# Gate and up on the second half of the tokens: block 1 computed ahead of block 0

## The chip, the cores and the metric

The kernel runs on one core of a Trainium2 chip. The metric is the device time of one launch in microseconds (us), the median of several runs. One further launch was profiled; its page and its trace are read below.

## The reference, cut to what matters

One decoder layer on x of 1024 tokens by 1024 channels, all in float32: two token mixers (differential attention and a convolution module) with a gated merge, then a SwiGLU channel mixer. The change lies in the channel mixer:

```python
    h = rms_norm(x, ffn_norm_w[l])
    gt, up = jnp.split(h @ w_gate_up[l], 2, axis=-1)
    x = x + (jax.nn.silu(gt) * up) @ w_down[l]
```

The hidden width FF is 2816, so gate and up are 22 blocks of 128 columns each; h is 1024 by 1024.

## The kernel before, in words

**Precision.** Every matrix operand is held as two fp32r tiles, a rounded high part (a ScalarE cast, `split_hi`, line 120) and the rest (a VectorE subtraction, `split_lo`, line 125). A product takes three TensorE matmuls: high times high, high times low, low times high (`mm3`, lines 152 to 155; `product`, line 1611).

**Stages.** Input projections, convolution and attention, the two output projections, the merge and `w_out` come first. The last matmuls of `w_out` (tile `wo`) run at about 1095 to 1121 us of the span. Then the channel mixer starts: `rest_of_rows` normalizes and transposes token tiles 4 to 7 into `h2_hi` and `h2_lo` (`h_hi`, `h_lo` in the profile) while the first blocks run.

**Two plain blocks.** Blocks f = 0 and f = 1 of gate and up (`NSTD = 2`) are computed plainly, on tokens 0 to 511 (sb = 0) and on tokens 512 to 1023 (sb = 1). `gate(f, sb, w)` runs 24 matmuls into a `pg` bank and a Silu on ScalarE (line 1477, tile `fsg`); `up(f, sb, w, sg)` runs 24 more, multiplies on VectorE (line 1482) and stores the result (line 1484). The weights are W[0], W[1] (gate and up of block 0) and W[2], W[3] (gate and up of block 1). They are loaded once and used for both halves. W[0], W[1] and W[2] fill the three buffers of the `whi`/`wlo` pairs in the pool `wp`. W[3] has no place there: `fourth` (line 539) puts it into the memory of the later tile `T4h`.

**The other 20 blocks** use a scheme of seven half-size products in place of eight. It needs differences of the four quarters of h: `differences()` (line 1501) takes 16 VectorE subtractions (lines 1508 to 1511) and splits T1, T2, T3 and T4 into high and low parts, four casts and four subtractions each. T4 is written where W[3] lay, so it can be written only after the last matmul that reads `fourth`. For each block f, `prepare(f)` (line 1572) loads two raw weight tiles (`wraw`, two buffers, line 1578) and makes, on VectorE and ScalarE, the pairs A11/A12, S1/S2 and S3/S4 (each one `whi`/`wlo` buffer, so three for a block) and A22 (`sh`, `sl`). The sums behind S1 to S4 are lines 1593 to 1596 (tile `s`); A22 is split by lines 120 and 125. `pair(f, ...)` (line 1616) runs the seven products of 12 matmuls each: A11 and A12 with h, S2 with T2, S1 with T1, S3 with T3, S4 with h, A22 with T4. Between the products come short steps on ScalarE and VectorE: the copy of the first product (line 1623, tile `p`), which must be done before S2 times T2 adds into the same bank, then lines 1625, 1626, 1630 and so on. `weight_sums` (lines 514 to 523, tile `wd`) prepares the down projection at the same time, one piece a block.

**What sets the order.** A scheduler places the instructions of each engine; each engine then works through its own list in order, and so does the DMA queue of SyncE (SP). An instruction that waits holds up all that stand behind it on its engine. A `whi`/`wlo` or `wraw` buffer goes to the next user when its last reader is done. After the 20 blocks comes the down projection (line 497).

Of the kernel before, what the change touches and what calls it, by code (L numbers as in the profile page):

```python
# [57 lines left out]
def kernel(  # L58
# [53 lines left out]
    def nm(s):  # L112
        uid[0] += 1
        return f"{s}_{uid[0]}"
# [4 lines left out]
    def split_hi(dst, src):  # L119
        act.copy(dst, src)  # L120
# [3 lines left out]
    def split_lo(dst, src, hi):  # L124
        last_lo[0] = dve.tensor_tensor(dst, src, f32(hi), op=ALU.subtract).ins  # L125
# [243 lines left out]
    def gemm_T(w, mhi, mlo, sb, amid=None):  # L369

        o = pg()
        cs = slice(sb * 512, (sb + 1) * 512)
        for k in range(NKT):
            mm3(o[:], w[0][:, k, :], w[1][:, k, :], kt(mhi, k)[:, cs], kt(mlo, k)[:, cs], k == 0, k == NKT - 1)
            if amid is not None and k == NKT // 2 - 1:
                amid()
        return o
# [1090 lines left out]
    def rest_of_rows(t_):  # L1468
        with after(last_mm[0]):
            norm2(t_, r2[1], tr_second)  # L1470
# [3 lines left out]
    def gate(f, sb, w, amid=None):  # L1474
        og = gemm_T(w, h2_hi, h2_lo, sb, amid)
        sg = wp.tile([P, 512], F32, tag="sg", name=nm("fsg"), bufs=2)
        act.activation(sg[:], og[:], AF.Silu)
        return sg

    def up(f, sb, w, sg, amid=None):  # L1480
        ou = gemm_T(w, h2_hi, h2_lo, sb, amid)
        dve.tensor_tensor(sg[:], ou[:], sg[:], op=ALU.mult)
        z = f"{sb + 1}{f % 2 + 1}"
        nc.sync.dma_start(sd[z][0][:] if z in sd else g21_d[:], sg[:])

    W = [ws.next()]
    sg = gate(0, 0, W[0])
# [4 lines left out]
    sg = gate(1, 0, W[2], lambda: rest_of_rows(5))  # L1492
# [8 lines left out]
    def differences():  # L1501


        q = []
        for i in range(4):
            b11, b21 = xa[i][:, 0:512], xa[i][:, 512:1024]
            b12, b22 = xa[4 + i][:, 0:512], xa[4 + i][:, 512:1024]
            dve.tensor_tensor(b11, b12, b11, op=ALU.subtract)
            dve.tensor_tensor(b12, b22, b12, op=ALU.subtract)
            dve.tensor_tensor(b22, b22, b11, op=ALU.subtract)  # L1510
            dve.tensor_tensor(b21, b21, b22, op=ALU.subtract)
            q.append({2: b22, 1: b11, 3: b12, 4: b21})
        for z in (2, 1, 3, 4):
            for i in range(4):
                ts = slice(i * P, (i + 1) * P)
                src = q[i][z].rearrange("p (k s) -> p k s", s=P)
                split_hi(T[z][0][:, :, ts], src)
                split_lo(T[z][1][:, :, ts], src, T[z][0][:, :, ts])

    sg = gate(0, 1, W[0])  # L1520
    up(0, 1, W[1], sg)
    differences()
    sg = gate(1, 1, W[2])
    up(1, 1, W[3], sg)
    n2_ctx.close()
    xp_ctx.close()

# [229 lines left out]
```

## Time and profile before

| | us |
|---|---|
| median of 3 runs (lowest to highest) | 1768.91 (1768.19 to 1770.76) |
| the profiled execution | 1769.82 |
| its span | 1768.0 |
| TensorE (PE) busy | 1740.1 |
| VectorE (DVE) busy | 1273.1 |
| ScalarE (ACT) busy | 800.8 |

The profiled execution's time is 1.82 us longer than its span. TensorE is the engine that is nearly always busy, so its idle stretches are what to look for. In a timeline row stand the start, the duration, the engine, the line, the operation, output and inputs, a count, and in brackets the idle time of that engine just before, with what ended it. The start-to-start distance of two 512-column matmuls that run without a wait is 0.227 us, although each shows 0.39 us: they overlap. PEclk is the granted TensorE clock, 1.00 being full speed.

### The profile page before, as it was taken

What the parts mean: (1) busy time and instruction counts of PE and PEld (TensorE: products, weight loads), DVE (VectorE), ACT (ScalarE), POOL (GpSimd) and SP (SyncE); (2) the same over time, 40 slices, a digit from 0 to 9 for tenths busy, and PEclk for the clock granted to TensorE, in tenths of its full rate; (3) what the DMA queues carried; (4) which work ended last, traced back from release to release, by engine and by line L of the source; (5) the groups of instructions that cost most, each with busy time, mean ns of one, the idle gap of its engine ahead of it and who ended that gap; (6) DMA issues with size and microseconds to landing.
All of it is one profiled execution on the core that took longest, in us unless ns stands there. A gap on an engine that the chain in (4) does not pass through costs nothing.

```text
span 1768.0 us, 25005 instructions
## 1 busy us (share of the span) xinstructions
PE 1740.1 (98%) x8983; PEld 1484.6 (84%) x8983; DVE 1273.1 (72%) x2171; ACT 800.8 (45%) x1883; POOL 19.6 (1%) x92
## 2 busy tenths in 40 slices
PE   6999999999999999999999999999999999999999
PEld 5778898998999998987788888878888888888887
DVE  6598888998898888885677534867667666665544
ACT  5221141557767776754457313633333333333332
POOL 0000000000000000000000000000000000000000
PEclk9999999999999999999999999999999999999999
DMA  6337334235443244341973544224544544697663
GB/s 231 107 125 232 131 111 115 70 104 138 120 141 105 82 125 145 97 147 60 339 261 108 167 166 143 90 90 152 171 159 148 177 153 148 202 357 250 214 214 131
DMA packets 251110, 275.29 MB, mean 156 GB/s; under 512 B 16505, under 2 KB 166050, under 8 KB 250986
## 3 DMA queue, kind: packets, MB, share of 16 engines
q1 hardware_dynamic: 249130, 267.47, 47.0%
q0 software_dynamic: 1280, 4.91, 0.9%
q10 hardware_dynamic: 576, 1.31, 0.3%
q8 instruction: 71, 1.16, 0.3%
q14 instruction: 53, 0.43, 0.1%
HBM read 176.59 MB, written 78.68 MB: 144 GB/s over the span
## 4 chain that ended last, share of the span: by engine, by line
PE 91%; DMA 3%; DVE 2%; ACT 2%; issue 1%; SPq 0%; DVEq 0%; ACTq 0%
PE acc L1611 19%; PE pg L153 14%; PE pg L154 14%; PE pg L155 14%; PE acc L497 12%; PE pg L688 4%; PE sc L1053 2%; PE sc L1052 2%; PE pT L1088 2%; PE wo L154 2%; PE wo L153 2%; PE wo L155 2%; PE pW L155 1%; PE pW L153 1%; PE pW L154 1%
## 5 line engine op out<-in xcount | busy, mean ns | idle before, releaser
L569 DVE SCALAR_TENSOR_TENSOR acc<-u,cw,acc 128x1024 f32<-128x1024 f32 x240 | 306.9, 1279 | 2.9
L153 PE MATMUL pg<-hT_hi,whi 128*128 128x512 f32 x512 | 201.7, 394 | 0.5 <-ACT hT_hi L120 0.2
L154 PE MATMUL pg<-hT_lo,whi 128*128 128x512 f32 x512 | 200.9, 392 | 0.0
L155 PE MATMUL pg<-hT_hi,wlo 128*128 128x512 f32 x512 | 200.7, 392 | 0.0
L120 ACT CAST whi<-wraw 128x1024 fp32r<-128x1024 f32 x101 | 106.1, 1051 | 182.9 <-PE pg L154 99.5
L125 DVE TENSOR_TENSOR wlo<-wraw,whi 128x1024 fp32r<-128x1024 f32 x101 | 123.0, 1219 | 63.3 <-ACT whi L120 59.4
L125 DVE TENSOR_TENSOR wlo<-draw,whi 128x1024 fp32r<-128x1024 f32 x75 | 91.8, 1224 | 89.1 <-ACT whi L120 86.1
L153 PE MATMUL pg<-whi,hT_hi 128*128 128x256 f32 x512 | 146.0, 285 | 0.3 <-ACT jk L756 0.3
L155 PE MATMUL pg<-whi,hT_lo 128*128 128x256 f32 x512 | 145.8, 285 | 0.0
L154 PE MATMUL pg<-wlo,hT_hi 128*128 128x256 f32 x512 | 145.5, 284 | 0.0
L120 ACT CAST whi<-draw 128x1024 fp32r<-128x1024 f32 x75 | 79.1, 1055 | 129.5 <-PE acc L497 122.6
L1059 ACT ACTIVATE E<-E,mn 128x256 f32<-128x256 f32 (+7 forms) x128 | 99.6, 780 | 45.9 <-DVE mn L1054 44.7
L497 PE MATMUL acc<-wlo,whi 128*128 128x512 f32 x308 | 119.8, 389 | 0.0
L497 PE MATMUL acc<-whi,wlo 128*128 128x512 f32 x308 | 119.8, 389 | 0.0
L153 PEld LDWEIGHTS pg<-hT_hi,whi 128*128 128x128 f32 x512 | 96.2, 188 | 20.5 <-ACT sgg L603 0.7
L155 PEld LDWEIGHTS pg<-hT_hi,wlo 128*128 128x128 f32 x512 | 96.2, 188 | 19.1
L154 PEld LDWEIGHTS pg<-hT_lo,whi 128*128 128x128 f32 x512 | 96.2, 188 | 19.0 <-issue 0.6
L153 PEld LDWEIGHTS pg<-whi,hT_hi 128*128 128x128 f32 x512 | 97.7, 191 | 2.2 <-ACT jk L756 1.0
L154 PEld LDWEIGHTS pg<-wlo,hT_hi 128*128 128x128 f32 x512 | 97.7, 191 | 1.3
L155 PEld LDWEIGHTS pg<-whi,hT_lo 128*128 128x128 f32 x512 | 97.7, 191 | 0.4
L1611 PE MATMUL acc<-h_hi,whi 128*128 128x512 f32 x240 | 93.4, 389 | 0.0
L1611 PE MATMUL acc<-h_lo,whi 128*128 128x512 f32 x240 | 93.4, 389 | 0.0
(280 smaller groups left out, 4191.1 us busy)
## 6 DMA issues: line engine op xcount, KB each, us to landing
wraw<-in_w_gate_up_dram SPq DMA_DIRECT2D x44, 512.0 KB, 4.8
wraw<-in_w_in_dram SPq DMA_DIRECT2D x38, 512.0 KB, 4.2
qs<-qs SPq DMA_DIRECT2D x96, 128.0 KB, 2.3
wd<-in_w_down_dram SPq DMA_DIRECT2D x44, 256.0 KB, 3.2
tdT<-wd SPq DMA_DIRECT2D x88, 128.0 KB, 4.5
draw<-sdS SPq DMA_DIRECT2D x44, 256.0 KB, 2.6
draw<-tdT SPq DMA_DIRECT2D x44, 256.0 KB, 4.3
wraw<-in_w_in_dram SPq DMA_DIRECT2D x32, 256.0 KB, 3.4
```

What stands on the lines that cost most here:

```text
L120: act.copy(dst, src)
L125: last_lo[0] = dve.tensor_tensor(dst, src, f32(hi), op=ALU.subtract).ins
L153: pe.matmul(o, lh, rh, start=start, stop=False)
L154: pe.matmul(o, lh, rl, start=False, stop=False)
L155: last_mm[0] = pe.matmul(o, ll, rh, start=False, stop=stop).ins
L497: m = pe.matmul(o[s_][i][:], l_[:, ts], r_[:, 512:], start=start and j + y_ == 0, stop=j == n - 1 and y_ == 2, skip_group_check=not start,)
L569: dve.scalar_tensor_tensor(acc[0][:], us[c][:, t : t + S], cw[:, c, t : t + 1], acc[0][:], op0=ALU.mult, op1=ALU.add)
L688: last_mm[0] = pe.matmul(o[:], l_, r_, start=first and n_ == 0, stop=last and n_ == len(terms) - 1).ins
L1052: pe.matmul(o[:, :w], qh[:, qs], k, start=True, stop=False)
L1053: last_mm[0] = pe.matmul(o[:, :w], ql[:, qs], k, start=False, stop=True).ins
L1059: act.activation(e[:, :nk], e[:, :nk], AF.Exp, bias=mn[:, j : j + 1], scale=-1.0, accum_out=l[:, j : j + 1])
L1611: pe.matmul(o[:], a_[x_][:, k, :], b_[y_][:, k, :], start=start and k + x_ + y_ == 0, stop=k == 3 and x_ == 1, skip_group_check=not start,)
```

## The change

On the second half of the tokens, gate and up of block 1 are computed first, then `differences()` is written, then gate and up of block 0. No computation is added or left out.

```diff
+    sg = gate(1, 1, W[2])
+    up(1, 1, W[3], sg)
+    differences()
     sg = gate(0, 1, W[0])
     up(0, 1, W[1], sg)
-    differences()
-    sg = gate(1, 1, W[2])
-    up(1, 1, W[3], sg)
     n2_ctx.close()
```

On TensorE the second half now runs through W[2], W[3] (`fourth`), W[0], W[1], where it was W[0], W[1], W[2], W[3]. As before, two matmuls of block 2's first product stand after the second of these four groups and three after the third.

The first place is on VectorE, where the plain blocks end. `fsg_11837` is the multiplication of the third plain group pair (up of the block that comes first on the second half), `fsg_11939` that of the last; T4l are the low parts of T4.

```order
 L125 TENSOR_TENSOR T2l<-xa_10937,T2h 128x4x128
 L1482 TENSOR_TENSOR fsg_11837<-pg_11839,fsg_11837 128x512
-L1482 TENSOR_TENSOR fsg_11939<-pg_11941,fsg_11939 128x512
 L125 TENSOR_TENSOR T4l<-xa_10938,T4h 128x4x128
 L125 TENSOR_TENSOR T4l<-xa_10939,T4h 128x4x128
```

The last multiplication no longer stands ahead of T4 and of all that follows T4.

The second place is on VectorE some ten instructions later. `wlo_11988` is the low part of block 2's S1/S2, `wlo_11992` of its S3/S4, `wlo_12037` of block 3's A11/A12; `s_1749`, `s_1750` and `sl_12124` belong to block 3.

```order
 L125 TENSOR_TENSOR wlo_11988<-s_1733_11977,whi_11987 128x1024
-L125 TENSOR_TENSOR wlo_11992<-s_1734_11978,whi_11991 128x1024
-L125 TENSOR_TENSOR wlo_12037<-wraw_11999,whi_12036 128x1024
 L1593 TENSOR_TENSOR s_1749_12034<-wraw_12001 128x512
-L1595 TENSOR_TENSOR s_1750_12035<-wraw_11999,wraw_12001 128x512
 L125 TENSOR_TENSOR sl_12124<-wraw_12001,sh_12123 128x512
 L518 TENSOR_TENSOR wd_12127<-wd_12127 128x256
 L1594 TENSOR_TENSOR s_1749_12034<-s_1749_12034,wraw_11999 128x512
+L1482 TENSOR_TENSOR fsg_11939<-pg_11941,fsg_11939 128x512
+L125 TENSOR_TENSOR wlo_11992<-s_1734_11978,whi_11991 128x1024
```

The last multiplication and block 2's S3/S4 now stand behind four steps of the next blocks, of which the first needs the raw tile `wraw_12001`.

The third place is on ScalarE at the same time. `whi_11987` is the high part of block 2's S1/S2, `whi_11991` of S3/S4, `sh_12123` the high part of block 3's A22, made from `wraw_12001`; `p_1748_12018` is the copy of block 2's first product.

```order
 L120 CAST sh_11995<-wraw_11975 128x512
+L1477 ACTIVATE fsg_11939<-pg_11914 128x512
+L120 CAST whi_11987<-s_1733_11977 128x1024
+L120 CAST sh_12123<-wraw_12001 128x512
+L120 CAST whi_11991<-s_1734_11978 128x1024
 L1623 COPY p_1748_12018<-acc_12004 128x512
-L120 CAST whi_11987<-s_1733_11977 128x1024
+L120 CAST whi_12036<-wraw_11999 128x1024
 L1626 ACTIVATE p_1748_12018<-p_1748_12018 128x512
```

S1/S2 moved ahead of the copy of the first product, and so did a cast that waits for a load.

## Prediction

> **What bounds the kernel now.** I read the page first: which engine is busy, and which ends the run.
>
> ```profile
> PE 1740.1 (98%) x8983; PEld 1484.6 (84%) x8983; DVE 1273.1 (72%) x2171; ACT 800.8 (45%) x1883; POOL 19.6 (1%) x92
> PE 91%; DMA 3%; DVE 2%; ACT 2%; issue 1%; SPq 0%; DVEq 0%; ACTq 0%
> ```
>
> TensorE is the bound. A change of order can only gain where TensorE stands still or runs slowly, so next the busy time by stage around the change and behind it (columns: stretch, its length, PE, PEld, DVE, ACT, POOL busy, PEclk, DMA share, GB/s).
>
> ```profile
> 1121.00:1200.00 79.00, 76.37 (x344) 62.47 (x343) 60.11 (x104) 37.79 (x63) 0.00 (x0) 0.98 0.28 90
> 1200.00:1560.00 360.00, 359.92 (x1588) 297.79 (x1587) 237.18 (x358) 122.25 (x167) 0.00 (x0) 1.00 0.53 171
> ```
>
> In the stage of the change TensorE is idle for 2.6 us and its mean clock is below 1; behind it TensorE is busy for 359.92 of 360 us. So whatever TensorE gets back here is not waited away later: the end moves with it. The waits of TensorE name the one place, and the timeline shows it.
>
> ```profile
> PE acc L1611 <- ACT whi L120: 2.4, 1, 2.4
> ```
>
> ```profile
> 1169.69 0.39 PE L1611 MATMUL acc<-h_hi,wlo 128*128 128x512 f32 x1
> ...
> 1173.77 0.39 PE L1611 MATMUL acc<-h_hi,wlo 128*128 128x512 f32 x1
> 1176.58 0.50 PE L1611 MATMUL acc<-T2h,whi 128*128 128x512 f32 x1 [2.42 <-ACT whi L120]
> ...
> 1177.84 0.80 PE L1611 MATMUL acc<-T2h,wlo 128*128 128x512 f32 x1
> 1178.43 0.63 PE L1611 MATMUL acc<-T2h,whi 128*128 128x512 f32 x1
> ...
> 1180.99 0.46 PE L1611 MATMUL acc<-T2h,whi 128*128 128x512 f32 x1
> 1181.29 0.39 PE L1611 MATMUL acc<-T2l,whi 128*128 128x512 f32 x1
> ...
> 1184.04 0.39 PE L1611 MATMUL acc<-h_hi,whi 128*128 128x512 f32 x1
> ```
>
> Block 2's first two products end at 1174.0 (1173.77 + 0.227), and the next product cannot start until 1176.58, since the high part of S1/S2 is late. Then a second loss: from 1177.84 to 1181.29 eight matmuls take 3.45 us where 1.81 us is usual (8 x 0.227). The stage table, cut finer, says why.
>
> ```profile
> 1163.00:1169.00 6.00, 6.00 (x28) 4.96 (x27) 0.00 (x0) 0.60 (x1) 0.00 (x0) 1.00 0.00 0
> 1169.00:1172.00 3.00, 3.00 (x15) 2.48 (x14) 2.06 (x4) 2.11 (x5) 0.00 (x0) 1.00 0.18 69
> ...
> 1174.00:1176.50 2.50, 0.16 (x1) 0.00 (x0) 2.50 (x5) 1.02 (x2) 0.00 (x0) 1.00 0.22 70
> 1177.80:1179.50 1.70, 1.66 (x4) 1.38 (x5) 1.22 (x1) 0.65 (x2) 0.00 (x0) 0.50 0.75 204
> 1179.50:1181.00 1.50, 1.50 (x5) 1.13 (x5) 0.88 (x1) 0.59 (x1) 0.00 (x0) 0.50 0.60 174
> ```
>
> After the idle stretch the granted clock is halved for about 3.3 us. The whole loss: from 1169.69 to 1184.04 stand 43 matmuls (19 of the first two products, 24 of S1 and S2), 43 x 0.227 = 9.75 us, but 14.35 us pass. **Loss 4.6 us**: 2.6 of idle, 1.65 of half clock, 0.35 of a refill and a short wait for `wlo` at 1177.84.
>
> Who made S1/S2 late? ScalarE and VectorE in the same microseconds:
>
> ```profile
> 1169.89 2.19 ACT L120 CAST T4h<-xa 128x512 fp32r<-128x512 f32 x4 [5.52 <-PE pg L155]
> 1171.98 0.62 ACT L120 CAST sh<-wraw 128x512 fp32r<-128x512 f32 x1
> 1175.48 1.05 ACT L120 CAST whi<-s 128x1024 fp32r<-128x1024 f32 x1 [2.41 <-DVE s L1594]
> ```
>
> ```profile
> 1158.70 0.68 DVE L1482 TENSOR_TENSOR fsg<-pg,fsg 128x512 f32<-128x512 f32 x1
> 1169.94 0.69 DVE L1482 TENSOR_TENSOR fsg<-pg,fsg 128x512 f32<-128x512 f32 x1 [10.57 <-issue]
> 1170.55 2.49 DVE L125 TENSOR_TENSOR T4l<-xa,T4h 128x512 fp32r<-128x512 f32 x4
> 1172.96 0.68 DVE L1593 TENSOR_TENSOR s<-wraw 128x512 f32<-128x512 f32 x1
> 1173.56 0.68 DVE L1595 TENSOR_TENSOR s<-wraw,wraw 128x512 f32<-128x512 f32 x1
> 1174.16 0.68 DVE L125 TENSOR_TENSOR sl<-wraw,sh 128x512 fp32r<-128x512 f32 x1
> 1174.77 0.68 DVE L1594 TENSOR_TENSOR s<-s,wraw 128x512 f32<-128x512 f32 x1
> 1175.97 0.68 DVE L1596 TENSOR_TENSOR s<-wraw,s 128x512 f32<-128x512 f32 x1
> 1176.57 1.22 DVE L125 TENSOR_TENSOR wlo<-s,whi 128x1024 fp32r<-128x1024 f32 x1
> ```
>
> VectorE idles 10.57 us, then works without a gap from 1169.94: the last multiplication, four T4 parts, then the sums, in steps of 0.6 us. All of it starts when the last plain group has been multiplied, because that group reads `fourth`, which lies where T4 goes, and its `fsg` stands at the head of the queue. The sums need nothing of it; they stand behind it.
>
> **The change, part by part.** Where TensorE stands between the four plain groups:
>
> ```profile
> 1157.67 0.39 PE L1611 MATMUL acc<-h_hi,whi 128*128 128x512 f32 x1
> 1163.57 0.39 PE L1611 MATMUL acc<-h_hi,wlo 128*128 128x512 f32 x1
> ```
>
> The groups end at 1157.67 (second), 1163.57 (third) and 1169.69 (fourth). All have 24 matmuls, so these times stay; no matmul is added or removed, and the swap itself costs nothing: the four weight tiles were all made for the first half.
>
> *T4 and the sums move forward.* `fourth` is now read last at 1157.45, one step before 1157.67. Before, T4h began 0.43 us after that matmul (its last was at 1169.46, one step before 1169.69; T4h at 1169.89). So T4h runs from 1157.9 to 1160.1 on a ScalarE that was waiting. VectorE is free at 1159.3, 0.6 after the 1158.70 row; four T4 parts end at 1161.7, and L1593, L1595, `sl`, L1594, L1596 follow to 1164.7. That is 11.25 us earlier for the first of them (1172.96 to 1161.7), in the idle 10.57 us.
>
> *S1/S2.* Its buffer is now the one of W[0], read until 1163.57, and its cast stands behind the Silu of that group: 1163.8 + 0.6 = 1164.4, cast until 1165.4, low part until 1166.7. TensorE asks for the high part at 1169.69 + 19 x 0.227 = 1174.0 and for the low part two matmuls on. Margins of 8.6 and 7.8 us: the 2.6 us wait goes, and with it what followed from it. **Minus 4.6 us** by this execution.
>
> *Multiplication, store and S3/S4 move back.* S3/S4 takes W[1]'s buffer, free only at 1169.9, and stands on ScalarE behind `sh_12123` and on VectorE behind `s_1749`; both wait for block 3's second raw tile. So does the last `fsg`, which nobody needs soon (its bank and its store have no reader in the next blocks). What stands behind that load on ScalarE is the copy of block 2's first product, on VectorE `wlo` of block 3's A11/A12. The load is priced by its rows of now:
>
> ```profile
> 1174.87 9.32 SPq L1578 DMA_DIRECT2D wraw<-in_w_gate_up_dram  x3
> ```
>
> ```profile
> 1181.84 0.62 ACT L120 CAST sh<-wraw 128x512 fp32r<-128x512 f32 x1 [1.75 <-DMA wraw<-in_w_gate_up_dram]
> ```
>
> ```profile
> DMA to landing us min/median/max: 2.9/4.2/8.4
> ```
>
> The first of three issues comes as `sl` ends (1174.84). I put the second at the end of L1596 (1176.65), which frees its buffer; used at 1181.84, that is 5.2 us. After the change L1596 ends at 1164.8, so the tile is there at 1170.0. ScalarE: `sh` 0.5, S3/S4 1.0, copy 0.6, done at 1172.1; T2's first matmul needs it at 1174.0 + 10 x 0.227 = 1176.3 (T1's first ten now go first). Margin 4.2 us. VectorE from 1170.0 to the end of `wlo_12037`: seven half-width steps of 0.6, two wide ones of 1.2, and three `wd` steps,
>
> ```profile
> 1183.72 0.42 DVE L518 TENSOR_TENSOR wd<-wd 128x256 f32<-128x256 f32 x1
> ```
>
> at about 0.35, in all 7.6: 1177.6. TensorE asks for it after the 24 matmuls of S1/S2 and four more, 1174.0 + 28 x 0.227 = 1180.35. Margin 2.7 us. It would be gone with a landing of 7.9 us, and the longest in the trace, 8.4, would cost 0.5 us. S3/S4 itself is ready at 1174, needed after 1183. Cost taken: 0; bounds 0 to 0.5 us. A gain beyond 4.6 is excluded: of the stage's 79.00 - 76.37 = 2.63 us of idle TensorE, 2.42 are this stretch.
>
> **Sum.** 1769.82 - 4.6 = 1765.2 for the profiled execution; its time lies 0.9 above the median of the runs, and from the median it is 1764.3. How far the half clock is in the median run is not known (below); I take **1764.9**, 4.0 us or 0.23% below 1768.91.
>
> [...] Three idle stretches of similar length:
>
> ```profile
> 28.49 1.29 PE L673 MATMUL px<-ident,xt 128*128 128x128 f32 x8 [2.17 <-DVE xt L667]
> 819.74 1.94 PE L1088 MATMUL pT<-ident,E 128*128 128x128 f32 x8 [3.15 <-DVE E L1068]
> ...
> 28.00:30.00 2.00, 1.47 (x10) 1.25 (x11) 1.83 (x4) 0.77 (x2) 0.00 (x0) 1.00 0.24 76
> 820.00:825.00 5.00, 4.88 (x23) 4.48 (x22) 2.04 (x4) 2.40 (x8) 0.20 (x1) 0.50 0.34 114
> ```
>
> After 2.17 us the clock stayed at 1.00, after 2.42 and 3.15 it was 0.50. So 2.42 us is near the point where it turns, and another execution may go the other way. [...]
>
> **Rivals.**
> 1. *The 2.42 us of idle do not halve the clock in the median run of before:* the gain is 4.6 - 1.65 = 2.95 us, 1766.0, within 0.2%. For it: the 2.17 row, and runs that spread over 2.6 us, more than 1.65. Against it: the profiled execution has it, and the idle is longer than 2.17. [...]
> 2. *The change gives back what it gains.* The buffer or the queue makes S1/S2 or block 3's A11/A12 late, TensorE waits 1 to 4 us in 1170 to 1185: 1767 to 1769. Against it: margins of 7.8 and 2.7 us. A version of it is that S1/S2 was late for another reason; but ScalarE's wait names L1594, and that step stood in an unbroken queue.
> 3. *Slower.* The load of `wraw_12001` now holds both queues. If it lands more than 7.9 us after its buffer is free, block 3's A11/A12 is late by the excess; to pass the old loss of 4.6 by 3.6 us, with 1.65 of half clock, the excess must be 6.5 us: a landing of 14.4 us, 1772.5. Against it: 8.4 is the longest of all landings, and the DMA engines have little else to do there (a share of 0.00 from 1163 to 1169, 0.18 to 1172).
>
> **How the numbers follow.** About 0.2% (3.5 us) is what a measurement of this kernel can tell from no change. Forecast (4.6 us or most of it, 1763.6 to 1765.4): 0.57. Rival 1: 0.31, rival 2: 0.08, both within 0.2%: 0.39. Rival 3: 0.04. The range: at the low end 4.6 off the lowest run and 0.3 for scatter, 1763.3; at the high end rival 1 from a run 1.2 above it, 1767.2; left out are rivals 2 and 3 and the tails, near 0.2.
>
> **What would show it.** Right: no TensorE wait at `acc` L1611 near 1174, clock 1.00 throughout 1170 to 1185, T4h at about 1158, the S1/S2 cast at about 1164.4, the 1184.04 matmul at about 1179.4. Wrong: a new wait at block 3's first product (1179 to 1181) or at T2's first matmul, `sh_12123` later than 1172, or a time of 1768 or more although the wait is gone, which would mean that the 4.6 us is lost again behind it.

## The result and the profile after

| | before | after |
|---|---|---|
| median of 7 runs on the same chip (lowest to highest) | 1770.76 us (1768.19 to 1772.96) | 1765.62 us (1763.01 to 1767.34) |
| profiled execution: time, span | 1769.82, 1768.0 us | 1765.62, 1763.6 us |
| the 43 matmuls of block 2's first products and S1/S2, in the profiled execution | 14.35 us | 9.75 us |

The measured ratio of after to before is 0.9974, 95% interval 0.9963 to 0.9985: 4.6 us faster, with 2.7 to 6.5 us as the interval (the shares times 1770.76; the two medians in the table are 5.1 us apart). A second measurement of the same kernel gave 0.9970, interval 0.9961 to 0.9979 (medians 1765.28 us against 1769.91). All gains below are worked out from such a ratio and the median of the kernel before that was measured beside it.

The page after: TensorE is still the bound, busy for 99% of the span, and the VectorE share of the chain that ended last fell from 2% to 1%.

```profile
PE 1737.5 (99%) x8983; PEld 1483.2 (84%) x8983; DVE 1273.4 (72%) x2171; ACT 802.9 (46%) x1883; POOL 19.6 (1%) x92
PE 93%; DMA 3%; ACT 2%; DVE 1%; issue 0%; SPq 0%; ACTq 0%
```

The stages around and behind the change, after (columns as before: stretch, length, PE, PEld, DVE, ACT, POOL busy, PEclk, DMA share, GB/s):

```profile
1121.00:1200.00 79.00, 78.86 (x364) 65.29 (x363) 63.36 (x110) 39.76 (x68) 0.00 (x0) 1.00 0.31 97
1200.00:1560.00 360.00, 359.94 (x1588) 297.74 (x1587) 238.16 (x357) 122.50 (x167) 0.00 (x0) 1.00 0.53 174
1160.00:1190.00 30.00, 30.00 (x134) 24.86 (x133) 17.71 (x28) 9.16 (x14) 0.00 (x0) 1.00 0.46 141
```

In the stage of the change the idle of TensorE went from 2.63 to 0.14 us and its mean clock from 0.98 to 1.00; behind it TensorE is as full as before (359.94 of 360). TensorE's timeline after, at the place where it stood still:

```profile
1169.87 0.39 PE L1611 MATMUL acc<-h_hi,wlo 128*128 128x512 f32 x1
...
1173.95 0.39 PE L1611 MATMUL acc<-h_hi,wlo 128*128 128x512 f32 x1
1174.18 0.39 PE L1611 MATMUL acc<-T1h,whi 128*128 128x512 f32 x1
...
1179.62 0.39 PE L1611 MATMUL acc<-h_hi,whi 128*128 128x512 f32 x1
```

The first S1/S2 matmul follows the last of the products at the usual 0.23 us. From 1169.87 to 1179.62 are 9.75 us for 43 matmuls, the bare work. ScalarE and VectorE after, as far as they lead there:

```profile
1158.06 2.19 ACT L120 CAST T4h<-xa 128x512 fp32r<-128x512 f32 x4 [2.56 <-PE pg L155]
...
1164.44 1.04 ACT L120 CAST whi<-s 128x1024 fp32r<-128x1024 f32 x1
1169.84 0.62 ACT L120 CAST sh<-wraw 128x512 fp32r<-128x512 f32 x1 [4.36 <-DMA wraw<-in_w_gate_up_dram]
...
1171.71 0.59 ACT L1623 COPY p<-acc 128x512 f32<-128x512 f32 x1 [0.29 <-PE acc L1611]
```

```profile
1158.88 0.69 DVE L1482 TENSOR_TENSOR fsg<-pg,fsg 128x512 f32<-128x512 f32 x1
1159.48 2.49 DVE L125 TENSOR_TENSOR T4l<-xa,T4h 128x512 fp32r<-128x512 f32 x4
1161.88 0.69 DVE L1593 TENSOR_TENSOR s<-wraw 128x512 f32<-128x512 f32 x1
...
1164.41 0.69 DVE L1596 TENSOR_TENSOR s<-wraw,s 128x512 f32<-128x512 f32 x1
1165.52 1.23 DVE L125 TENSOR_TENSOR wlo<-s,whi 128x1024 fp32r<-128x1024 f32 x1 [0.42 <-ACT whi L120]
1170.27 0.69 DVE L1593 TENSOR_TENSOR s<-wraw 128x512 f32<-128x512 f32 x1 [3.52 <-DMA wraw<-in_w_gate_up_dram]
...
1176.62 1.22 DVE L125 TENSOR_TENSOR wlo<-wraw,whi 128x1024 fp32r<-128x1024 f32 x1
```

The sums start at 1161.88, not 1172.96, and S1/S2 is ready at 1166.7 (1165.52 + 1.23). The two waits for block 3's raw tile are there (in brackets at the end of the rows of 1169.84 and 1170.27), and the last row, block 3's A11/A12, ends at 1177.84, before TensorE asks for it at 1180.5 (1174.18 + 28 x 0.227).

### The profile page after: what moved, and what is told of

Read it like the earlier page. It is cut to its first block, busy times and chain, and to the rows that moved or that the text cites. A ratio compares the mean times of both kernels' runs of the same rounds, so it can differ in the third digit from the quotient of the medians.

```text
span 1763.6 us, 25012 instructions
## 1 busy us (share of the span) xinstructions
PE 1737.5 (99%) x8983; PEld 1483.2 (84%) x8983; DVE 1273.4 (72%) x2171; ACT 802.9 (46%) x1883; POOL 19.6 (1%) x92
## 4 chain that ended last, share of the span: by engine, by line
PE 93%; DMA 3%; ACT 2%; DVE 1%; issue 0%; SPq 0%; ACTq 0%
PE acc L1611 21%; PE pg L153 14%; PE pg L154 14%; PE pg L155 14%; PE acc L497 12%; PE pg L688 4%; PE sc L1053 2%; PE sc L1052 2%; PE pT L1088 2%; PE wo L154 2%; PE wo L153 2%; PE wo L155 2%; PE pW L155 1%; PE pW L153 1%; PE pW L154 1%; DMA xt<-in_x_dram 1%
```

## The experiments

The theory: S1/S2 was late because its sums stand on VectorE behind T4, and T4 behind the last reading of `fourth`. The rivals: the gain comes from something else that the order of the blocks changes; the half clock behind the wait was a matter of one execution; the moved load takes part of the gain back.

**The order kept, the memory changed.** The kernel before, except that it is the second block's gate tile W[2], not its up tile W[3], that lies in T4's memory. It is then last read when gate is through, one group earlier; the order of the blocks is that of before.

```diff
-        ws.plan(ld_cols(wgu, f * P) + ld_cols(wgu, FF + f * P, *([fourth] if f == 1 else [])))
+        ws.plan(ld_cols(wgu, f * P, *([fourth] if f == 1 else [])) + ld_cols(wgu, FF + f * P))
```

> The order of before (block 0 first on the second half), but the weight tile that lies in T4h's memory is W[2], the gate of block 1, and W[3] goes to the pool; so the last reader of that memory ends at about 1163.6 us of the span, where it was 1169.7 before and 1157.6 after. Theory (what counts is when T4's memory is free, not which block comes first): T4h from about 1163.9, the S1/S2 cast from about 1169.3, done by 1170.4, asked for at 1174.0: no wait at the S1/S2 product, no half clock in 1170 to 1185, the whole gain, 4.4 to 4.6 us below before. Rival (the order of the blocks itself is what gains): no gain, within 0.1% of before, with the 2.4 us wait.

Measured: 1765.79 us against 1769.58, ratio 0.9981 (0.9973 to 0.9990), 3.4 us faster (1.8 to 4.8). Its ScalarE and VectorE:

```profile
1163.02 2.19 ACT L120 CAST T4h<-xa 128x512 fp32r<-128x512 f32 x4 [8.46 <-PE pg L155]
...
1168.62 2.00 ACT L120 CAST whi<-s 128x1024 fp32r<-128x1024 f32 x2 [2.41 <-DVE s L1594]
```

```profile
1163.68 2.50 DVE L125 TENSOR_TENSOR T4l<-xa,T4h 128x512 fp32r<-128x512 f32 x4 [5.03 <-ACT T4h L120]
1166.10 0.69 DVE L1593 TENSOR_TENSOR s<-wraw 128x512 f32<-128x512 f32 x1
```

```profile
1160.00:1190.00 30.00, 30.00 (x134) 24.84 (x133) 20.13 (x30) 12.37 (x19) 0.00 (x0) 1.00 0.44 134
```

T4 moves to 1163.0, 5.0 us later than in after and 6.9 earlier than in before (1169.89), and that is enough: TensorE is busy for the whole 30 us at full clock, as in after. The gain does not need the blocks exchanged; letting `fourth` go earlier is enough.

**The new order of the blocks, `fourth` last all the same.** The kernel after, with the second block's gate first but its up, which reads `fourth`, at the end.

```diff
-    sg = gate(1, 1, W[2])
-    up(1, 1, W[3], sg)
-    differences()
+    sg1 = gate(1, 1, W[2])
     sg = gate(0, 1, W[0])
+    differences()
     up(0, 1, W[1], sg)
+    up(1, 1, W[3], sg1)
```

> As after, block 1 comes first with its gate, but its up (W[3], in T4h's memory) is moved to the end: gate of block 1, gate of block 0, up of block 0, up of block 1. Theory: T4h cannot start before about 1169.9, the S1/S2 cast not before about 1175.5, the 2.4 us wait comes back, and the time is that of before (a gain of 0 within 0.1%). Rival (the order of the blocks itself): most of the 4.6 us gain is kept.

Measured: 1767.46 us, ratio 0.9989 (0.9981 to 0.9998), 1.9 us faster (0.4 to 3.4). That interval alone does not decide between theory and rival; the trace does. T4 and the cast of S1/S2 are late again, and the wait and the half clock are back:

```profile
1168.83 2.19 ACT L120 CAST T4h<-xa 128x512 fp32r<-128x512 f32 x4 [10.73 <-PE pg L155]
...
1174.42 1.04 ACT L120 CAST whi<-s 128x1024 fp32r<-128x1024 f32 x1 [2.40 <-DVE s L1594]
```

```profile
1177.80:1179.50 1.70, 1.70 (x6) 1.31 (x5) 0.77 (x2) 1.05 (x1) 0.00 (x0) 0.50 0.82 237
```

The wait is shorter than before, though:

```profile
1168.63 0.39 PE L1611 MATMUL acc<-h_hi,wlo 128*128 128x512 f32 x1
...
1173.39 0.39 PE L1611 MATMUL acc<-h_hi,wlo 128*128 128x512 f32 x1
1175.52 0.50 PE L1611 MATMUL acc<-T2h,whi 128*128 128x512 f32 x1 [1.74 <-ACT whi L120]
...
1183.07 0.39 PE L1611 MATMUL acc<-h_hi,whi 128*128 128x512 f32 x1
```

From 1168.63 to 1173.39 are 22 matmuls where before had 19 (1169.69 to 1173.77): in this order the three matmuls of block 2's first product that stood between the third and the fourth plain group stand behind the fourth. They take 0.68 us, and the wait is shorter by just that (2.42 to 1.74). The whole stretch of 46 matmuls takes 14.44 us against 10.43 of work: a loss of 4.0 us where before had 4.6. So 0.6 us was to be gained and not 0; the expectation missed these three matmuls. 0.6 lies inside the measured interval, and what would make up the rest of its middle, 1.9 us, is not shown.

**S1/S2 made late again, in the kernel after.** In block 2 only, L1594 is done 8 or 12 times more (the diff shows 8; `range(13)` for 12), over the same data, which puts 0.72 us of VectorE each (seven of them took 5.04 us) between T4 and S1/S2.

```diff
-        dve.tensor_tensor(s12[:, 512:1024], s12[:, 0:512], a11, op=ALU.subtract)
+        for _ in range(9 if f == NSTD else 1): dve.tensor_tensor(s12[:, 512:1024], s12[:, 0:512], a11, op=ALU.subtract)
```

> After, with the second of the four sums for block 2 (line 1594) written 8 more times over itself, same values, 0.6 us each on VectorE: S1/S2 is made about 8 us later. Theory (the margin of S1/S2 is 8 to 9 us, so nothing of this delay reaches TensorE): the same time as after within 0.1%, a wait of at most 0.3 us at the S1/S2 product. Rival (the margin is not there, since the queue also holds the last multiplication): a wait of over 1 us and 1 to 4 us longer than after.

> After, with the same sum written 12 more times over itself, about 2.5 us beyond the margin. Theory (late sums alone make the loss): a wait of 2 to 3 us at the S1/S2 product and, when the clock is halved behind it, 1.6 us more: 3 to 5 us longer than after, so about the time of before although the block order is that of after. If a wait of this length does not halve the clock, 2.5 to 3.3 us longer. Rival (the block order makes the gain): within 1 us of after.

Measured: with 8 more 1765.2 us, ratio 0.9978 (0.9970 to 0.9987), the gain still there; with 12 more 1770.13 us, ratio 1.0003 (0.9995 to 1.0012), all of it gone. With 8 more, ScalarE casts S1/S2 from 1170.17 to 1171.2 (the row holds S3/S4 as well), a microsecond before TensorE asks for it, and TensorE stays full:

```profile
1170.17 2.00 ACT L120 CAST whi<-s 128x1024 fp32r<-128x1024 f32 x2
```

```profile
1172.17 0.39 PE L1611 MATMUL acc<-T2h,whi 128*128 128x512 f32 x1
```

```profile
1160.00:1190.00 30.00, 30.00 (x134) 24.86 (x133) 23.07 (x35) 10.56 (x14) 0.00 (x0) 1.00 0.42 129
```

With 12 more, the cast comes at 1176.12, and TensorE stands still and then runs at half clock:

```profile
1176.12 1.99 ACT L120 CAST whi<-s 128x1024 fp32r<-128x1024 f32 x2
```

```profile
1170.22 0.39 PE L1611 MATMUL acc<-h_hi,wlo 128*128 128x512 f32 x1
...
1177.21 0.52 PE L1611 MATMUL acc<-T2h,whi 128*128 128x512 f32 x1 [2.53 <-ACT whi L120]
```

```profile
1177.80:1179.50 1.70, 1.70 (x5) 1.29 (x5) 1.70 (x3) 1.25 (x2) 0.00 (x0) 0.50 0.81 240
...
1160.00:1190.00 30.00, 27.47 (x114) 22.21 (x113) 24.09 (x36) 8.47 (x13) 0.00 (x0) 0.94 0.37 113
```

The same 43 matmuls take 14.2 us (1170.22 to 1184.42), a loss of 4.45 us. Late sums, in the new order and with T4 early (it starts at 1158.40), bring the loss back. Two things did not stay as in after: with 8 and with 12 more, the copy of the first product stands ahead of S1/S2 on ScalarE again, and TensorE begins with S2 again, as in before. Neither made the wait: with 12 more the copy was done at 1172.6, and the cast began when the last of the repeated steps ended. That the step from nothing to everything lies between 8 and 12 doesn't measure the margin exactly: in both kernels the last multiplication waits for TensorE (1.4 us) among the repeated steps, and with 12 more a step on the first product (L1625) comes ahead of the last of them.

**Before again, three times.** The kernel before, unchanged, one execution each, for the half clock.

> The kernel before, unchanged, one look. The question is whether the clock is halved behind the 2.4 us wait in every execution. The forecast had 0.57 for a gain of 3.5 us or more, which needs the half clock in most executions: about 3.3 us at 0.50 from about 1177, a loss of 4.6 us between the fourth plain group and 43 matmuls on. Rival 1: clock 1.00 behind the wait in half of the looks or more, and a loss of 2.9 to 3.0 us there.

> The kernel before once more, second look: half clock behind the wait and a loss of 4.6 us there (forecast), or clock 1.00 and 2.9 to 3.0 us (rival 1).

> The kernel before once more, third look: half clock behind the wait and a loss of 4.6 us there (forecast), or clock 1.00 and 2.9 to 3.0 us (rival 1).

Measured: 1767.78, 1769.58 and 1768.84 us. The same 43 matmuls take 14.26, 14.26 and 14.44 us, a loss of 4.5, 4.5 and 4.7. The first of the three, the matmul that waited and the ones in which the clock falls and rises again, and its stage:

```profile
1175.04 0.50 PE L1611 MATMUL acc<-T2h,whi 128*128 128x512 f32 x1 [2.42 <-ACT whi L120]
...
1176.30 0.79 PE L1611 MATMUL acc<-T2h,wlo 128*128 128x512 f32 x1
1176.89 0.63 PE L1611 MATMUL acc<-T2h,whi 128*128 128x512 f32 x1
1177.32 0.63 PE L1611 MATMUL acc<-T2l,whi 128*128 128x512 f32 x1
...
1179.02 0.58 PE L1611 MATMUL acc<-T2h,wlo 128*128 128x512 f32 x1
1179.44 0.39 PE L1611 MATMUL acc<-T2h,whi 128*128 128x512 f32 x1
```

```profile
1160.00:1190.00 30.00, 27.58 (x114) 22.03 (x113) 15.96 (x24) 10.58 (x16) 0.00 (x0) 0.94 0.37 114
```

The other two have the wait of 2.42 us and the clock of 0.94 in this stretch too. With the execution that the prediction was made from, four of four show the half clock.

**After again.** The kernel after, unchanged.

> The changed kernel once more beside the looks at before, for the scatter of its time. Theory: no wait and clock 1.00 in 1170 to 1185 again, time 4 to 5 us below before. The stretch from 815 to 832 us, which the change does not touch, shows how much of the scatter is the clock behind another wait: clock 0.80 there in both first profiles; if the scatter of the runs comes from such stretches, it is another value here when the time is another.

Measured: the second ratio above, 5.3 us faster (3.7 to 6.9). Its profiled execution took 1766.75 us, and its stage is full again:

```profile
1160.00:1190.00 30.00, 30.00 (x134) 24.86 (x133) 19.16 (x30) 10.45 (x16) 0.00 (x0) 1.00 0.45 141
```

## Why the prediction was right

- **Loss of 4.6 us at S1/S2, gone.** Forecast 4.6 from one execution; the 43 matmuls went from 14.35 to 9.75 us, and the spans differ by 4.4 (after reached the start of the stretch 0.18 us later, 1169.87 against 1169.69). The two measured gains, 4.6 and 5.3 us, agree with it.
- **T4 and the sums move forward.** Forecast T4h at 1157.9, L1593 at 1161.7, the cast at 1164.4; seen at 1158.06, 1161.88 and 1164.44. That it was the queue behind `fourth` is shown in two ways: letting `fourth` go earlier in the old order gives the gain, and reading it last in the new order brings the wait back. That the new order gains by the earlier sums is shown by the kernels in which they are late: with 12 more steps the gain is gone, at a ratio of 1.0003 (0.9995 to 1.0012), which leaves at most 0.9 us for anything else that the order brings.
- **The margin of 8.6 us.** Borne out: with 8 repeated steps the cast ended 1.0 us before it was asked for (1171.2 against 1172.17), so 7.6 us of it were used up at no cost. With 12 the cast ended at 1177.1, 2.6 us after TensorE was through with the products (1170.22 + 19 x 0.227 = 1174.5), and there was a wait of that size.
- **The load that both queues now wait for.** Forecast landed at 1170.0, seen at 1169.84, 4.7 us after the end of L1596 where 5.2 was put (4.7 in the second profiled execution of after too); copy of the first product done at 1172.1, seen at 1172.3 (1171.71 + 0.59), and what it waited for last was TensorE, not the load; `wlo_12037` ready at 1177.6, seen at 1177.84. Cost forecast 0, and TensorE shows none: it never waits there. The 8.4 us that the prediction called the longest of all landings is the longest of the loads into `wraw` only; the loads into `xa` took 10.1 us in the median in the same trace. And in the trace after, loads into `wraw` take up to 9.8 us elsewhere:

```profile
DMA to landing us min/median/max: 2.9/4.3/9.8
```

  At this place one of 9.8 in place of 4.7 would be 2.4 us past the margin of 2.7. Rival 3 was thus not excluded by the size of landings, only by this load's own; a slower load was not tried.
- **Rival 1, the half clock as a matter of chance.** It had the largest chance beside the forecast, and at this place it fell: the clock is halved in all four profiled executions of before, and behind the shorter wait of 1.74 us too. The prediction was too careful: it took 0.6 us off the gain for it (1764.9 where its own sum from the median gave 1764.3). Its picture of a length near which the clock turns doesn't hold either. The wait near 28 us on which it leaned is 2.17 to 2.21 us long in all ten profiled executions; in nine the clock behind it stayed at 1.00, in the second one of after it was 0.50 from 30 to 32 us. A wait of 2.02 to 2.21 us near 16 us had half clock behind it in all four executions that show it. So chance does play a part elsewhere in this kernel, and a rare execution without half clock here is not excluded: of 50 further runs of before, timed beside the experiments, one had a mean clock of 0.999, in 1764.91 us, and the others 0.994 to 0.998. Which stretch at half clock it lacked isn't known without a trace.
- **The gain without the half clock.** Waits of 1.74, 2.42 and 2.53 us were each followed by a clock of 0.50. Without the half clock the gain would have been 2.95 us (rival 1); the two measured ratios leave 2.7 to 6.5 and 3.7 to 6.9 us, so the second excludes it.
- **The size in us.** The median after is 1765.62 where 1764.9 was forecast. That is no sign of a missed term, for over all seven runs the kernel before has a median of 1770.76, against the 1768.91 of three runs that the forecast started from. The interval of the gain, 2.7 to 6.5 us, can't tell the 4.0 us forecast from the 4.6 us of the trace.

## What to carry to other kernels

When a queue that is in program order stands idle and then works without a gap, look at what its first instruction waits for, and whether the late result behind it needs that at all: here VectorE stood idle for 10.57 us, and the sums only stood behind T4. Shared memory is an edge of the schedule like any other, and the read that lets go of it can be moved by exchanging two blocks or by choosing another tile to share. A wait of TensorE cost more than its length here, so look at the granted clock behind it in more than one execution: 2.4 us of idle cost 4.5 to 4.7 us, of which 1.7 us were the half clock, while waits of 2.17 to 2.21 us near 28 us had none in nine of ten executions.

## What the runs showed that was not expected

- **Half clock behind waits of 1.74 to 2.53 us.** Six of six executions with a wait of 1.74 to 2.53 us at this place had the half clock behind it. It lasted 3.4 us in each of the six (the clock that is missing, summed over stretches of 1 us, is 1.70 to 1.71 us), but doesn't begin at a fixed point: the first matmul at half rate started 1.8 us after the end of the wait with 1.74 us (1177.36 against 1175.52), 0.3 us after it with 2.53 (1177.55 against 1177.21). What sets the point at which it begins can't be read from these traces. The shortest wait with half clock behind it is one of 1.49 us near 17 us, with 0.22 us more a little later, in the second execution of after; five other executions had 1.49 us there and kept a clock of 1.00.
- **The same at another wait makes part of the scatter.** Behind the wait of 3.15 us near 820 us, which the change doesn't touch, the clock of this stretch was 0.80 in four of the ten profiled executions: the first ones of before and after, the one with the memory changed and the one with 8 more steps. After:

```profile
815.00:832.00 17.00, 13.73 (x69) 11.96 (x68) 6.02 (x10) 6.71 (x16) 0.46 (x3) 0.80 0.15 46
```

  In the other six, among them the second one of after and all three further ones of before, it was 0.90. The second one of after:

```profile
815.00:832.00 17.00, 13.44 (x81) 11.78 (x80) 6.62 (x12) 6.71 (x16) 0.57 (x3) 0.90 0.15 46
```

  That is 6.8 or 3.4 us at half clock (a fifth or a tenth of 17 us, doubled). From this wait to the first matmul of `w_out` TensorE took 210.0 to 210.6 us in the four executions with 0.80, and 208.8 to 209.3 in five of the six with 0.90 (210.1 in the sixth): about 1.2 us of the 4.3 and 4.8 us over which the seven runs of each kernel spread.

  It doesn't say which execution is the longer one, as the last expectation supposed: the second execution of after had 0.90 here and took 1.1 us longer than the first. It had come to this wait 3.0 us late (823.25 us, the first 820.21). Some 1.8 us of that were lost in the first 60 us, where it ran at half clock twice and the first execution once (the rows of the first and of the second):

```profile
0.00:60.00 60.00, 44.75 (x207) 35.63 (x208) 36.94 (x75) 29.72 (x50) 2.31 (x12) 0.97 0.57 196
0.00:60.00 60.00, 45.07 (x199) 35.59 (x200) 37.00 (x75) 29.68 (x50) 2.32 (x12) 0.94 0.57 196
```

  Behind that it waited 1.69 us for a load near 531 us, where the first execution waited 0.28 us (the waits of the second in sum, their number, and the longest):

```profile
PE pW L155 <- DMA vl<-v_lo: 1.8, 2, 1.7
```
